# Transformer layer on one core: modulation columns summed over partitions by transposes and a VectorE reduction

## The chip, the cores and the metric

The kernel runs on one core of a Trainium2 chip. The metric is the time of one execution on the device in microseconds (us). Of the kernel before, three runs gave a median of 2660.23 us (2659.34 to 2661.08). The engines are called PE (TensorE, matmuls), PEld (its weight loads), DVE (VectorE), ACT (ScalarE), POOL (GpSimd) and SP (SyncE, which issues the DMAs here).

## The reference, cut to what matters

One layer works on 1024 latent tokens and 256 context tokens of width 1024: a half-step SwiGLU, two attentions side by side, a merge, another half-step SwiGLU. Every sub-layer is modulated by columns that come from two conditioning vectors, `c` for the latent tokens and `c_ctx` for the context tokens:

```python
m  = jnp.split((silu(c) @ w_ada + b_ada)[:, None, :], 9, axis=-1)   # w_ada: 1024 x 9216
mc = jnp.split(silu(c_ctx) @ w_ada + b_ada, 9, axis=-1)
...
x  = x + 0.5 * m[2] * rmsnorm(swiglu(rmsnorm(x) * (1 + m[1]) + m[0]))
```

Each `m[i]` is a vector-matrix product over 1024 rows of `w_ada`, 1024 outputs. `mc` is needed for i = 0 to 4 only, since the context tokens end in the attention. All of it is fp32.

## The kernel before, in words

Every large product of the kernel is done as three matmuls on a high and a low part of each fp32 operand (`mm3`), and the SwiGLU products are further cut into seven products of half size instead of eight (`Unit`, `Down7`). The program runs through a list of steps (`Plan`): `main` holds PE work, one step being for example 12 matmuls of 128x512, and `side` holds other work that is issued right behind a given main step. `plan.spread(steps, first, last)` lays a list of side steps evenly over the main steps `first` to `last`. The order so written is the order on every engine's queue; each engine takes its queue in order, and SP issues the loads and stores in the same order.

The modulation columns m = 0 and 1 are made at the start by PE (`Ada`). The others, m = 2 to 8, are made by DVE beside the large products (`AdaSum`). For one m, the weight rows are loaded in 16 pieces of 128x512 (k = 0 to 7, half h = 0 or 1). For each piece DVE multiplies by the conditioning value of the partition and adds to an accumulator `acc[v][h]` (v = 0 latent, v = 1 context, which only m < 5 has). After eight k an accumulator holds, for 512 outputs, 128 partial sums, one in each partition, and these must be added over the partitions and laid out as a column, output on the partition. That last step is `AdaSum.end`: in the kernel before it is one product per 128 outputs, with 128x128 of the accumulator as the weights and the column `ones` (part of the tile `strip`) as the moving operand; the result is one column of a PSUM bank `bv`. So m = 2, 3, 4 take 16 products each and m = 5 to 8 take 8 each, 80 in all. DVE then adds the bias `bada` and writes `mod[m]`.

`ada_steps` writes the side steps of some m: 18 steps with loads and accumulations, two empty ones, and `end`. m = 2 lies beside the first SwiGLU's up-products, m = 4 and 3 beside its down-products, m = 5, 6, 7 beside the projections that `lat_tile` makes, m = 8 beside the second SwiGLU's down-products.

PSUM has eight banks, in three tags: `bs` and `bm` with three buffers, `bv` with two. `bv` serves the fifth and third products of a `Unit` (`p5`, `p3`), two of eight tiles of `Down`, and `AdaSum.end`. `turn_` is a transpose on PE: `ident` is the identity, `x` the 128x128 block.

Of the kernel before, what the change touches and what calls it, by code (L numbers as in the profile page):

```python
# [12 lines left out]
ALU = mybir.AluOpType  # L13
AX = mybir.AxisListType

P = 128
# [5 lines left out]
KD = D // P  # L22
# [21 lines left out]
def hybrid_block(ctx: ExitStack, tc: tile.TileContext, a: dict, out: bass.AP):  # L44
# [11 lines left out]
    def nm(s):  # L56
        count[0] += 1
        return f"{s}_{count[0]}"
# [8 lines left out]
    def U(dt=F32, key="u"):  # L67
        return pools[key].tile([P, 1024], dt, tag="u", name=nm("x" + key))
# [7 lines left out]
    def T2(dt=F32, n=512):  # L76
        return pools["t"].tile([P, n], dt, tag="t", name=nm("t"))

    def ST(n=1):
        return sp.tile([P, n], F32, tag=f"st{n}", name=nm("st"))  # L80
# [7 lines left out]
    def PB(tag):  # L88
        return ps.tile([P, 512], F32, tag=tag, name=nm("b" + tag), bufs=PBUFS[tag])
# [8 lines left out]
    def const(name, shape, src=None, dt=F32):  # L98
        t = cp.tile(shape, dt, tag=name, name=name)
        if src is not None:  # L100
            ld(t, src)
        return t
# [4 lines left out]
    def pin(i):  # L107
        if pinned[0]:
            tc.keep_in_program_order(i)
        return i  # L110
# [39 lines left out]
    vec, act, pool = Engine(nc.vector), Engine(nc.scalar), Engine(nc.gpsimd)  # L150

    def mmul(o, s, m, start, stop):
        return pin(nc.tensor.matmul(o, s, m, start=start, stop=stop, skip_group_check=open_group[0]))  # L153

    def turn_(o, x, i):
        return pin(nc.tensor.transpose(o, x, i))  # L156
# [64 lines left out]
    ident = const("ident", [P, P])  # L221
    bada = const("bada", [P, 9, KD])
# [14 lines left out]
    ones = strip[:, 1:2]  # L237
# [7 lines left out]
    mod = [const(f"mod{m}", [P, 2, KD]) for m in range(9)]  # L245

    class Ada:
# [16 lines left out]
        def end(self):  # L264
            self.rows = T2()
            vec.tensor_copy(self.rows[:, :256], self.bank[:, :256])
            self.turn()
# [11 lines left out]
    class AdaSum(Ada):  # L279
# [16 lines left out]
                else:  # L296
                    vec.scalar_tensor_tensor(t[h], r, sc[:, k, v:v + 1], t[h], op0=ALU.mult, op1=ALU.add)

        def end(self):

            pb = PB("v")
            n = len(self.acc)
            for v, t in enumerate(self.acc):
                for k in range(KD):
                    mmul(pb[:, v * KD + k:v * KD + k + 1], t[k // 4][:, (k % 4) * P:(k % 4 + 1) * P], ones, True, True)
            for v in range(n):
                vec.tensor_tensor(mod[self.m][:, v, :], pb[:, v * KD:(v + 1) * KD], bada[:, self.m, :], op=ALU.add)

    cols = {}

    def ada_steps(ms):

        s = []
        cur = {}

        def step(m, k, h):
            if m not in cur:
                cur[m] = AdaSum(m)
            if k:
                cur[m].step(k - 1, h)  # L320
            if k < KD:
                cur[m].load(k, h)

        def end(m):
            cur[m].end()
            if m == 4:
                cols["a1"] = scale_col("a1", 4, 2, 2)
            if m == 7:
                cols["a2"] = scale_col("a2", 7, 4, 1)

        for m in ms:
            s += [lambda m=m, k=k, h=h: step(m, k, h) for k in range(KD + 1) for h in range(2)]
            s += [lambda: None] * 2 + [lambda m=m: end(m)]
        return s

    def scale_col(name, m, g, nv):
        t = const(name, [P, 2, KD])
        for v in range(nv):
            vec.scalar_tensor_tensor(t[:, v, :], mod[m][:, v, :], 1.0, ng[:, g, :], op0=ALU.add, op1=ALU.mult)
        return t  # L340
# [734 lines left out]
    e = len(plan.main)  # L1075
# [7 lines left out]
    rest1 = len(plan.main)  # L1083
    plan_rest(plan, units1)
    plan.spread(ada_steps((2,)), rest1 + 10, len(plan.main) - 10)


# [45 lines left out]
    for i, d in enumerate(downs):  # L1133
        last = i == len(downs) - 1
# [15 lines left out]
        e = len(plan.main)  # L1150
# [3 lines left out]
        if i < len(downs) - 2:  # L1154
            n = downs[i + 1]
            plan.spread([lambda n=n: n.loads(n.fs[0])], o, o + 1)
            plan.spread(n.steps(), o + 3, e)
        elif not last:
            n = downs[i + 1]
# [3 lines left out]
    for x, (p, f, w) in enumerate(ctx_at):  # L1163
# [3 lines left out]
        plan.spread([lambda f=f, w=w, e=e: ctx_split(f, w, e) for e in range(2)], q, max(q + 1, q1))  # L1167
    dstart = ctx_at[0][0] - 5
    plan.spread(ada_steps((4, 3)), dstart + 14, ctx_at[-4][0] - 6)

    gcol = {}
# [98 lines left out]
    e = len(plan.main)  # L1270
# [127 lines left out]
    for x, (c, s, ts) in enumerate(sets):  # L1398
# [5 lines left out]
        if x + 1 < len(sets):  # L1404
            plan.spread(sets[x + 1][1].loads(), o, o + 1)
            plan.spread(sets[x + 1][1].steps(), o + 1, len(plan.main))
    va_at = o
    plan.spread(ada_steps((5, 6, 7)), lat_at + 1, va_at - 2)

    def rotate(x, cc, ss, nh):  # L1410
# [470 lines left out]
    for e in range(2):  # L1881
        e = U(F32R)
# [204 lines left out]
    e = len(plan.main)  # L2087
# [118 lines left out]
```

## Time and profile before

| | |
|---|---|
| median of the runs shown | 2660.23 us |
| time of the profiled execution | 2662.05 us |
| its span in the profile | 2660.0 us |
| PE busy | 2609.1 us, 98% |
| PEld busy (beside PE) | 2234.1 us, 84% |
| DVE busy | 1847.5 us, 69% |
| ACT busy | 1171.9 us, 44% |
| mean granted PE clock | 0.994 |

The span is what the profile shows of the execution, 2.05 us less than the time of that execution. A row of the timeline gives the start, the length, the engine, the line, the operation and its tiles, how many instructions were merged into it, and in brackets the idle time ahead of it with what ended it. Buffer numbers are left out of the tile names. Matmuls overlap, so the time that a group of them takes on PE is read from its start to the start of the next group, not from its length. In rows of windows the number behind the engines' busy times is the granted PE clock, 1.00 being full speed. An fp32 matmul of `ones` appears as two passes (two weight loads and two matmuls), a transpose as one.

### The profile page before, as it was taken

What the parts mean: (1) busy time and instruction counts of PE and PEld (TensorE: products, weight loads), DVE (VectorE), ACT (ScalarE), POOL (GpSimd) and SP (SyncE); (2) the same over time, 40 slices, a digit from 0 to 9 for tenths busy, and PEclk for the clock granted to TensorE, in tenths of its full rate; (3) what the DMA queues carried; (4) which work ended last, traced back from release to release, by engine and by line L of the source; (5) the groups of instructions that cost most, each with busy time, mean ns of one, the idle gap of its engine ahead of it and who ended that gap; (6) DMA issues with size and microseconds to landing.
All of it is one profiled execution on the core that took longest, in us unless ns stands there. A gap on an engine that the chain in (4) does not pass through costs nothing.

```text
span 2660.0 us, 38323 instructions
## 1 busy us (share of the span) xinstructions
PE 2609.1 (98%) x13690; PEld 2234.1 (84%) x13690; DVE 1847.5 (69%) x3495; ACT 1171.9 (44%) x2248; POOL 227.9 (9%) x380
## 2 busy tenths in 40 slices
PE   7999999999999999999999999999999999999998
PEld 5888888888888788789888999998788888888887
DVE  4777875586866676675366998886625788778557
ACT  4532223531323663331355988875246422234533
POOL 0000000000000400000101432221011000000001
PEclk9999999999999999999999999999999999999999
DMA  7454433453433564477879953214224566546755
GB/s 287 154 165 147 140 123 106 141 171 113 160 111 119 185 217 168 159 246 227 234 269 271 258 142 74 74 30 171 99 92 167 185 238 229 186 167 246 276 184 196
DMA packets 220430, 460.58 MB, mean 173 GB/s; under 512 B 25488, under 2 KB 64592, under 8 KB 220240
## 3 DMA queue, kind: packets, MB, share of 16 engines
q1 hardware_dynamic: 220240, 458.14, 52.2%
q8 instruction: 108, 1.77, 0.3%
q14 instruction: 82, 0.67, 0.1%
HBM read 338.71 MB, written 119.34 MB: 172 GB/s over the span
## 4 chain that ended last, share of the span: by engine, by line
PE 53%; issue 33%; DVE 6%; ACT 5%; DMA 2%; POOL 1%; SPq 0%; DVEq 0%; POOLq 0%; ACTq 0%
PE bs L153 24%; PE bm L153 15%; PE bv L153 11%; PE bm L156 2%; ACT xu L1833 1%; DVE t L120 1%; DVE xu L1700 1%; DVE xv L120 1%; ACT t L120 1%; DVE xu L120 1%; POOL st L120 1%; ACT t L1859 1%; ACT xu L120 1%; DVE t L1860 1%; PE bs L156 1%
## 5 line engine op out<-in xcount | busy, mean ns | idle before, releaser
L153 PE MATMUL bm<-xu,xu 128*128 128x512 f32 (+1 forms) x2271 | 553.1, 388 | 1.4 <-DVE xu L120 1.1
L153 PEld LDWEIGHTS bm<-xu,xu 128*128 128x128 f32 x2271 | 419.8, 189 | 83.9 <-DVE xu L120 1.9
L153 PE MATMUL bs<-xu,xu 128*128 128x512 f32 (+1 forms) x1875 | 461.4, 386 | 0.5 <-DVE xu L120 0.4
L120 ACT CAST xu<-t 128x512 fp32r<-128x512 f32 x402 | 238.5, 617 | 388.9 <-DVE t L120 333.4
L153 PEld LDWEIGHTS bs<-xu,xu 128*128 128x128 f32 x1875 | 348.1, 189 | 68.2 <-DVE xu L120 0.8
L120 DVE TENSOR_TENSOR xu<-t,xu 128x512 fp32r<-128x512 f32 x402 | 265.7, 686 | 142.4 <-ACT xu L120 142.4
L153 PE MATMUL bs<-xv,xu 128*128 128x512 f32 (+1 forms) x1488 | 356.0, 389 | 5.1 <-DVE t L120 5.0
L153 PEld LDWEIGHTS bs<-xv,xu 128*128 128x128 f32 x1488 | 279.5, 189 | 63.0 <-issue 7.1
L153 PE MATMUL bv<-xv,xu 128*128 128x512 f32 x1276 | 318.5, 389 | 0.0
L153 PEld LDWEIGHTS bv<-xv,xu 128*128 128x128 f32 x1276 | 239.6, 188 | 49.8
L120 POOL TENSOR_SCALAR st<-st 128x1 f32<-128x1 f32 x72 | 37.8, 525 | 2077.6 <-ACT t L120 2017.9
L153 PE MATMUL bs<-w,w 96*128 96x512 f32 (+3 forms) x832 | 206.1, 366 | 7.7 <-DVE st L1725 7.1
L120 DVE TENSOR_TENSOR xu<-xu,xu 128x512 fp32r<-128x512 f32 (+2 forms) x219 | 149.3, 687 | 76.4 <-ACT xu L120 74.3
L153 PE MATMUL bm<-t,xu 128*128 128x256 f32 (+1 forms) x1272 | 167.4, 289 | 0.6 <-ACT t L120 0.4
L153 PEld LDWEIGHTS bm<-t,xu 128*128 128x128 f32 x1272 | 162.3, 193 | 5.7 <-ACT t L120 0.8
L120 DVE TENSOR_TENSOR xu<-xv,xu 128x512 fp32r<-128x512 f32 (+2 forms) x184 | 131.3, 738 | 48.1 <-ACT xu L120 45.0
L120 DVE TENSOR_TENSOR t<-t,t 128x512 f32<-128x512 f32 (+2 forms) x222 | 142.3, 642 | 25.8 <-ACT t L120 23.0
L153 PE MATMUL bv<-t,w 128*128 128x256 f32 x896 | 151.1, 288 | 5.0 <-ACT t L1859 1.7
L153 PEld LDWEIGHTS bv<-t,w 128*128 128x128 f32 x896 | 132.6, 189 | 20.6 <-DVE t L1860 4.9
L153 PE MATMUL bv<-xu,xu 128*128 128x512 f32 x530 | 143.4, 391 | 0.0
L120 ACT CAST xu<-xu 128x512 fp32r<-128x512 f32 (+2 forms) x211 | 127.9, 617 | 28.8 <-DMA xu<-in_wc 15.0
L153 PEld LDWEIGHTS bs<-w,w 96*128 96x128 f32 (+1 forms) x832 | 123.2, 190 | 17.1 <-DVE st L1725 10.1
(192 smaller groups left out, 3583.2 us busy)
## 6 DMA issues: line engine op xcount, KB each, us to landing
d<-t SPq DMA_DIRECT2D x321, 256.0 KB, 2.5
t<-d SPq DMA_DIRECT2D x204, 256.0 KB, 5.1
xu<-in_f1w SPq DMA_DIRECT2D x64, 512.0 KB, 4.1
xv<-in_f1w SPq DMA_DIRECT2D x64, 512.0 KB, 3.6
xu<-in_f2w SPq DMA_DIRECT2D x58, 512.0 KB, 4.6
t<-in_wada SPq DMA_DIRECT2D x112, 256.0 KB, 3.9
w<-d SPq DMA_DIRECT2D x112, 256.0 KB, 6.3
xv<-d SPq DMA_DIRECT2D x42, 512.0 KB, 5.4
```

The source lines that it names most:

```text
L120: return lambda *x, **y: pin(f(*x, **y))
L153: return pin(nc.tensor.matmul(o, s, m, start=start, stop=stop, skip_group_check=open_group[0]))
L156: return pin(nc.tensor.transpose(o, x, i))
L1700: nc.vector.tensor_scalar(dst, src, 1.0, FMIN, op0=ALU.mult, op1=ALU.max, accum_out=m)
L1833: nc.scalar.activation(x, x, AF.Exp, bias=n_[:, s:s + 1], accum_out=l[:, i:i + 1])
L1859: nc.scalar.copy(t[0], pb)
L1860: nc.vector.tensor_tensor(t[1], pb, f32(t[0]), op=ALU.subtract)
```

## The change

`AdaSum.end` takes one accumulator half at a time. Four transposes write the four 128x128 blocks of `acc[v][h]` into a `bv` bank, DVE sums each block along the free axis (`tensor_reduce`, 128x512 to 128x4) into a small tile `st`, and adds the bias into four columns of `mod[m]`. `ada_steps` makes a side step of each half: four for m = 2, 3, 4 and two for m = 5 to 8, where there was one. The lists of side steps grow from 21 to 24 (m = 2), 42 to 48 (m = 4, 3), 63 to 66 (m = 5, 6, 7) and 21 to 22 (m = 8), and each is still laid over the same main steps.

```diff
-        def end(self):
-            pb = PB("v")
-            n = len(self.acc)
-            for v, t in enumerate(self.acc):
-                for k in range(KD):
-                    mmul(pb[:, v * KD + k:v * KD + k + 1], t[k // 4][:, (k % 4) * P:(k % 4 + 1) * P], ones, True, True)
-            for v in range(n):
-                vec.tensor_tensor(mod[self.m][:, v, :], pb[:, v * KD:(v + 1) * KD], bada[:, self.m, :], op=ALU.add)
+        def end(self, v, h):
+            pb, s = PB("v"), ST(4)
+            for k in range(4):
+                turn_(pb[:, k * P:(k + 1) * P], self.acc[v][h][:, k * P:(k + 1) * P], ident)
+            vec.tensor_reduce(s, pb.rearrange("p (k c) -> p k c", k=4), axis=AX.X, op=ALU.add)
+            vec.tensor_tensor(mod[self.m][:, v, 4 * h:4 * h + 4], s, bada[:, self.m, 4 * h:4 * h + 4], op=ALU.add)
...
         for m in ms:
             s += [lambda m=m, k=k, h=h: step(m, k, h) for k in range(KD + 1) for h in range(2)]
-            s += [lambda: None] * 2 + [lambda m=m: end(m)]
+            ends = [(v, h) for v in range(2 if m < 5 else 1) for h in range(2)]
+            s += [lambda: None] * 2 + [lambda m=m, e=e: end(m, *e, e == ends[-1]) for e in ends]
```

On PE, at the end of m = 8 in the second SwiGLU's down-products (`bs` and `bm` with `xu` are those products, three to a row; the numbers only name tiles), the order before is:

```order
L153 MATMUL bs_23911<-xu_24325,xu_24322 128x512 x3
L153 MATMUL bm_23912<-xu_24325,xu_24322 128x512 x3
L153 MATMUL bv_24399<-strip,t_23960 128x1 x4
L153 MATMUL bv_24399<-strip,t_23961 128x1 x4
L153 MATMUL bs_23909<-xu_24348,xu_24345 128x512 x3
L153 MATMUL bm_23910<-xu_24348,xu_24345 128x512 x3
```

and now:

```order
L153 MATMUL bm_23969<-xu_24359,xu_24356 128x512 x3
L156 MATMUL bv_24434<-ident,t_24017 128x128 x4
L153 MATMUL bs_23966<-xu_24383,xu_24380 128x512 x3
L153 MATMUL bm_23967<-xu_24383,xu_24380 128x512 x3
L153 MATMUL bs_23968<-xu_24383,xu_24380 128x512 x3
L153 MATMUL bm_23969<-xu_24383,xu_24380 128x512 x3
L156 MATMUL bv_24464<-ident,t_24018 128x128 x4
```

The eight products with `strip` in one place have become two groups of four transposes, with a main step of twelve matmuls between them. For m = 2, 3 and 4 the sixteen products become four such groups, one to four main steps apart.

On DVE, at the end of m = 2 in the first SwiGLU's up-products, the order before is:

```order
L120 TENSOR_TENSOR xu_3499<-t_3481,xu_3499 128x512
L120 TENSOR_TENSOR xu_3502<-xu_3349,xu_3502 128x512
L120 TENSOR_TENSOR mod_102<-bv_3507,bada 128x8 x2
L120 TENSOR_TENSOR t_3556<-bs_3543,t_3540 128x512
L120 TENSOR_TENSOR t_3558<-xu_3349,t_3455 128x512
```

and at the first of the four new ends:

```order
L120 TENSOR_TENSOR t_3266<-bs_3253,t_3250 128x512
L120 TENSOR_TENSOR t_3268<-xu_3110,t_3185 128x512
L120 TENSOR_TENSOR xu_3270<-xu_3129,xu_3270 128x512
L120 TENSOR_REDUCE st_3274<-bv_3273 128x4
L120 TENSOR_TENSOR mod_102<-st_3274,bada 128x4
L120 TENSOR_TENSOR t_3309<-bv_3296,t_3250 128x512
```

The reduction of 512 elements per partition stands on DVE's queue four times where two additions of 8 elements stood once; the first row of the last piece already reads the PE step (`bs_3253`) behind which the transposes are placed.

More of the change, by code (lines that the diff above doesn't have):

```diff
@@ L322, in step, with end @@
                 cur[m].load(k, h)
-        def end(m):
-            cur[m].end()
-            if m == 4:
+        def end(m, v, h, last):
+            cur[m].end(v, h)
+            if last and m == 4:
                 cols["a1"] = scale_col("a1", 4, 2, 2)
-            if m == 7:
+            if last and m == 7:
                 cols["a2"] = scale_col("a2", 7, 4, 1)
```

## The prediction

> **What bounds the kernel now.** I read the page first: the busy times, the slices and the chain.
>
> ```profile
> PE 2609.1 (98%) x13690; PEld 2234.1 (84%) x13690; DVE 1847.5 (69%) x3495; ACT 1171.9 (44%) x2248; POOL 227.9 (9%) x380
> PE   7999999999999999999999999999999999999998
> PE 53%; issue 33%; DVE 6%; ACT 5%; DMA 2%; POOL 1%; SPq 0%; DVEq 0%; POOLq 0%; ACTq 0%
> ```
>
> PE is full in every slice but the first and last, and the chain runs over PE's own queue. So time taken off PE comes off the span, wherever it lies, unless PE then waits for what it did not wait for; time added to the others costs nothing as long as PE still finds its inputs. Second view: the products with the column of ones, by their tile.
>
> ```profile
> L153 PE MATMUL bv<-strip,t x176: 164/250/353, 86.0 to 2492.6; 128*128 128x1 f32 x176
>   DVE mod L120: 12.9, 7
> ```
>
> 176 passes are 88 fp32 products: 80 in the seven ends that change, 8 in `shift_cols`, which stays. The last row says who waited for them: DVE, 12.9 us in 7 waits; PE had no idle time ahead of them. Third view: PE's timeline around the ends.
>
> ```profile
> 419.22 2.88 PE L153 MATMUL bs<-xu,xu 128*128 128x512 f32 x12
> 421.94 4.21 PE L153 MATMUL bv<-strip,t 128*128 128x1 f32 x32
> 426.01 5.47 PE L153 MATMUL bm<-xu,xu 128*128 128x512 f32 x12
> 431.28 3.10 PE L153 MATMUL bs<-xv,xu 128*128 128x512 f32 x12
> 434.22 2.88 PE L153 MATMUL bm<-xu,xu 128*128 128x512 f32 x12
> ...
> 642.42 3.63 PE L153 MATMUL bv<-strip,t 128*128 128x1 f32 x32
> 645.91 2.29 PE L153 MATMUL bv<-xu,xu 128*128 128x512 f32 x6
> 648.00 2.51 PE L153 MATMUL bs<-xu,xu 128*128 128x512 f32 x6
> 650.35 1.53 PE L153 MATMUL bm<-xu,xu 128*128 128x512 f32 x6
> ...
> 786.46 3.63 PE L153 MATMUL bv<-strip,t 128*128 128x1 f32 x32
> 789.95 4.62 PE L153 MATMUL bm<-t,xu 128*128 128x256 f32 x24
> 797.15 3.04 PE L153 MATMUL bm<-t,xu 128*128 128x256 f32 x24
> ...
> 1194.53 3.33 PE L153 MATMUL bs<-xu,t 128*128 128x288 f32 x24
> 1197.70 1.84 PE L153 MATMUL bv<-strip,t 128*128 128x1 f32 x16
> 1199.40 3.41 PE L153 MATMUL bm<-xu,t 128*128 128x288 f32 x24
> 1202.64 4.00 PE L153 MATMUL bs<-xv,xu 128*128 128x352 f32 x24
> ...
> 2491.03 1.84 PE L153 MATMUL bv<-strip,t 128*128 128x1 f32 x16
> 2492.73 0.96 PE L153 MATMUL bs<-xu,xu 128*128 128x512 f32 x3
> 2493.52 0.85 PE L153 MATMUL bm<-xu,xu 128*128 128x512 f32 x3
> ```
>
> Two things are to be seen. An end of 16 products holds PE for 4.07 us (421.94 to 426.01) or 3.49 us, and one of 8 for 1.70 us. And the large matmuls behind an end of 16 are slow: twelve that otherwise take 2.72 us (419.22 to 421.94) take 5.27. The fourth view, windows, says why:
>
> ```profile
> 421.90:426.00 4.10, 4.10 (x33) 4.06 (x33) 3.87 (x7) 1.14 (x2) 0.00 (x0) 0.85 0.31 115
> 426.00:431.30 5.30, 5.30 (x14) 4.14 (x15) 0.24 (x2) 0.00 (x0) 0.00 (x0) 0.50 0.03 10
> 789.90:794.40 4.50, 4.50 (x26) 4.50 (x26) 0.24 (x2) 0.00 (x0) 0.00 (x0) 0.62 0.27 100
> 1199.40:1202.60 3.20, 3.20 (x26) 3.20 (x26) 0.17 (x1) 0.00 (x0) 0.00 (x0) 1.00 0.87 248
> ```
>
> The granted clock falls behind the ends of 16 (0.50 over the 5.3 us behind m = 2, a mean of 0.62 behind m = 3; behind m = 4 the matmuls slow down alike), and stays at 1.00 behind the end of 8 at 1197.70. So the 16-product ends cost twice, by themselves and by the clock.
>
> The Trainium skill ("TensorE: Matmul & The Clock Gate", Part 1) has the array fall to half its clock after an idle window of about 3.4 us; the rows agree on the length, but not on the word idle, since PE was executing throughout (4.10 of 4.10 us): 3.5 us of one-column products count as idle.
>
> **What is removed, from PE.** End by end, start to start, less what the large matmuls in the same stretch take at full clock:
> - m = 2: 421.94 to 434.22 is 12.28, less 2 x 2.72: 6.84 us.
> - m = 4: 642.42 to 650.35 is 7.93, less 2.72: 5.21 us.
> - m = 3: 3.49 for the products, and 4.62 instead of 3.04 for the group behind: 5.07 us.
> - m = 5: 1197.70 to 1202.64 is 4.94, less 3.17 (1194.53 to 1197.70): 1.77 us.
> - m = 8: 2491.03 to 2493.52 is 2.49, less 0.68 for three matmuls (a quarter of 2.72): 1.81 us.
> - m = 6 and 7 have the same 16 passes as m = 5; I take 1.79 each.
>
> Sum 24.3 us, of which the products are about 17.9 and the clock about 6.
>
> **What is added, on PE.** 80 transposes in groups of four, of which the order puts two groups back to back only at m = 6 and m = 7. The trace has such groups, made for the planes, inside the stream of large matmuls:
>
> ```profile
> 76.41 0.60 PE L156 MATMUL bs<-ident,xv 128*128 128x128 f32 x4
> 76.77 3.02 PE L153 MATMUL bm<-xu,xu 128*128 128x512 f32 x12
> 79.62 0.60 PE L156 MATMUL bs<-ident,xv 128*128 128x128 f32 x4
> ...
> 1301.05 0.60 PE L156 MATMUL bs<-ident,t 128*128 128x128 f32 x4
> 1301.48 0.60 PE L156 MATMUL bm<-ident,t 128*128 128x128 f32 x4
> 1301.84 3.00 PE L153 MATMUL bs<-xv,xv 128*128 128x512 f32 x12
> ...
> 76.40:86.00 9.60, 9.60 (x49) 7.99 (x48) 5.56 (x9) 4.86 (x8) 0.00 (x0) 1.00 0.52 170
> ```
>
> Four transposes and twelve matmuls repeat after 3.21 us (76.41 to 79.62), so a group costs 3.21 - 2.72 = 0.49 us; two groups together take 0.79 us themselves (1301.05 to 1301.84). 20 groups are 9.8 us, about 9.6 with the two pairs. The clock over three such rounds is 1.00, so no drop follows.
>
> The Trainium skill (the same page, Part 4) puts a transpose at about 275 ns in a kernel. Priced so, 80 of them are an estimated 22 us and nearly all of the gain is gone; the trace shows lengths that fit (the 0.60 us of four overlapped ones) but starts 0.09 us apart, and it is the starts that PE pays.
>
> **What is added, on DVE.** 20 reductions of 128x512 from PSUM, and 20 additions of 4 elements for 10 of 8. No such reduction is in the trace. Nearest rows:
>
> ```profile
> L120 DVE TENSOR_TENSOR t<-t,bs 128x512 f32<-128x512 f32 x112 | 76.5, 683 | 33.4 <-PE bs L153 33.3
> L1732 DVE TENSOR_REDUCE st<-st 128x2 f32<-128x4 f32 x32 | 4.8, 149 | 0.4
> L120 DVE TENSOR_TENSOR mod<-bv,bada 128x8 f32<-128x8 f32 x14 | 1.9, 163 | 13.9 <-PE bv L153 12.9 <-PE bv L156 1.1
> ```
>
> A reduction reads as many elements as the first row, and its output is as small as the second's: between 0.15 and 0.68 us. I take 0.68, since the rows of this kernel go by what is read. That makes 20 x 0.68 + 10 x 0.16 = 15.2 us more for DVE, none of it on PE's path by my sum. The cover is that DVE waits for PE in these stretches (33.3 us over the 112 additions of the first row), and stood waiting for the ones products themselves (12.9 us above). Each reduction stands on the queue behind a DVE instruction that reads the PE step just ahead of the transposes, so it waits only some 0.4 us for them (at m = 8 DVE reads no product in between and waits longer, as it does before). Behind it are queued the halves of weights that PE needs one to several steps (2.72 us each) later; a delay of 0.4 + 0.68 + 0.16 = 1.2 us stays below that. If the cover were gone, it would be 15 us (a rival below).
>
> **What moves.** Loads and accumulations are spread among 24 side steps where 21 were (66 where 63 were, 22 where 21 were), so each comes sooner, by an eighth of the stretch at most; their number, and that of the 112 loads of `in_wada` on SP's queue, is the same. A load stays two side steps ahead of its use. The 20 banks of `bv`, where 7 were, take turns with the products' own; the nearest reuse is that of a `Down` tile's bank two tiles and a group of transposes later, 2 x 1.36 + 0.49 = 3.2 us after its end, and DVE's addition that frees it takes 0.68 us. I cost both at nothing; a wait of one DVE instruction at every group would be 20 x 0.68 = 14 us at most.
>
> **Sum.** 24.3 - 9.6 = 14.7 us off the span of 2660.0. The profiled execution took 2662.05 us, 1.8 above the median of the runs; from the median 2660.2 I get 2645.5 us.
>
> What shakes it: the clock drops elsewhere too, behind short waits.
>
> ```profile
> 924.95 5.73 PE L153 MATMUL bm<-xu,t 128*128 128x512 f32 x24 [1.50 <-ACT t L120]
> 1120.27 4.57 PE L153 MATMUL bs<-xv,xu 128*128 128x512 f32 x12 [1.88 <-DVE t L120]
> ```
>
> After a wait of 1.88 us twelve matmuls took 4.57 instead of 2.88 us; after 1.50 us 24 took the usual time. Whether such a wait tips the clock looks like a matter of where it falls, and everything behind 422 us will now fall elsewhere: some two drops of 1.7 us more or fewer, so 3.4 us either way. The likeliest case's own range is 2641 to 2650.
>
> **Rivals.**
> - Slower: the transposes take the clock down, as one-column products do. The Trainium skill (same page, Part 4) says that transposes do not count as PE activity as other matmuls do. A drop costs at least 1.58 us (behind m = 3); behind all 20 groups that is 32 us, giving 2677, and it decides from the tenth group on (14.7 / 1.58 = 9.3). Against it: the 1.00 over the rounds of transposes above, and that 8 one-column products in 1.70 us did not drop it, four times as long as a group. Chance 0.03.
> - No change: DVE's 15.2 us, or the waits for banks, lie on PE's path, 2660. For it: PE sits at 98%, so any late input shows. Against it: DVE's waits for PE. Chance 0.05; the page's 275 ns for a transpose would land here too (24.3 - 22, 2658), and is in this chance.
> - Half the gain: the large matmuls behind m = 2, 4 and 3 are slow for another reason than the products ahead of them, and only those go: 17.9 - 9.6 = 8.3, 2652; a gain partly eaten by later waits ends here too. Chance 0.12.
> - The forecast: 0.80.
>
> **Numbers.** About 0.2% (5.3 us) is what a measurement of this kernel can tell from no change. The forecast and the half gain are both faster: 0.92; same 0.05; slower 0.03. The range of 2640 to 2653 holds the forecast with its clock drops and most of the half gain.
>
> **What would show it.** Right: no `strip` products behind 100 us, PE granted 1.00 throughout 420 to 435 and 640 to 655 us, 20 groups of four `ident,t` transposes that start some 0.4 us ahead of the next matmul, TENSOR_REDUCE rows of about 0.68 us, PE without idle time at the groups. Wrong: a clock of 0.5 behind a group, a wait of PE for `mod` or `st`, or PE rows of `bv` that wait for DVE.

## The result, and the profile after

The median is 2649.3 us (2647.57 to 2653.39, 6 runs) against 2661.37 us (2659.34 to 2663.9, 6 runs) before: 12.1 us less, ratio 0.9956 (95% interval 0.9944 to 0.9969). The profiled execution took 2648.12 us, its span is 2646.3 us, 13.7 us below the span before. The forecast was 2645.5 us, the range 2640 to 2653.

The page after, busy times:

```profile
PE 2596.5 (98%) x13610; PEld 2222.1 (84%) x13610; DVE 1861.2 (70%) x3525; ACT 1173.0 (44%) x2248; POOL 229.1 (9%) x380
```

PE has 12.6 us less to do, DVE 13.7 us more, and PE is as full as before. The groups of the reductions and of the transposes after (instructions, then us busy, mean ns, then idle time ahead):

```profile
L120 DVE TENSOR_REDUCE st<-bv 128x4 f32<-128x512 f32 x20 | 13.7, 685 | 5.1 <-PE bv L156 5.1
L156 PE MATMUL bv<-ident,t 128*128 128x128 f32 x84 | 12.5, 273 | 1.1 <-DVE t L120 1.1
```

The reduction takes 0.685 us. The 1.1 us of idle time at the transposes are at the four of `Ada` at the start (before 45 us); the 80 new ones have none. The timeline of PE after, at the first end of m = 2, and the granted clock where it had dropped, behind m = 2 and m = 4:

```profile
390.07 0.60 PE L156 MATMUL bv<-ident,t 128*128 128x128 f32 x4
390.43 2.99 PE L153 MATMUL bm<-xu,xu 128*128 128x512 f32 x12
393.26 2.88 PE L153 MATMUL bv<-xv,xu 128*128 128x512 f32 x12
...
424.10:432.00 7.90, 7.90 (x38) 6.59 (x37) 6.33 (x12) 2.25 (x4) 0.00 (x0) 1.00 0.18 66
640.00:648.00 8.00, 8.00 (x38) 6.62 (x37) 6.06 (x12) 0.00 (x0) 0.00 (x0) 1.00 0.27 100
```

A group costs 3.19 - 2.72 = 0.47 us, and the clock behind the ends is 1.00 (behind those of m = 3 too, 774 to 790 us). To see where the time went, both timelines are cut at rows that they share (the first and the last row of each list lie ahead of and behind all ends). Before:

```profile
86.02 1.84 PE L153 MATMUL bv<-strip,t 128*128 128x1 f32 x16
485.04 1.88 PE L153 MATMUL bm<-t,xu 128*128 128x256 f32 x6 [0.41 <-ACT t L120]
904.70 0.77 PE L156 MATMUL bs<-ident,xv 128*128 128x128 f32 x5 [3.44 <-ACT xv L120]
1137.61 4.58 PE L153 MATMUL bs<-xv,xu 128*128 128x512 f32 x12 [1.85 <-DVE t L120]
1361.76 1.64 PE L153 MATMUL bs<-xu,xu 128*128 128x512 f32 x6 [0.36 <-DVE xu L120]
2278.55 3.00 PE L153 MATMUL bs<-xv,xu 128*128 128x512 f32 x12 [0.38 <-DVE t L120]
2498.31 1.03 PE L156 MATMUL bv<-ident,st 128*128 128x128 f32 x8
```

After:

```profile
86.78 1.84 PE L153 MATMUL bv<-strip,t 128*128 128x1 f32 x16
480.88 1.88 PE L153 MATMUL bm<-t,xu 128*128 128x256 f32 x6 [0.43 <-ACT t L120]
894.07 1.33 PE L156 MATMUL bs<-ident,xv 128*128 128x128 f32 x5 [3.56 <-ACT xv L120]
1109.71 3.00 PE L153 MATMUL bs<-xv,xu 128*128 128x512 f32 x12 [1.89 <-DVE t L120]
1125.47 4.58 PE L153 MATMUL bs<-xv,xu 128*128 128x512 f32 x12 [1.88 <-DVE t L120]
1347.01 1.63 PE L153 MATMUL bs<-xu,xu 128*128 128x512 f32 x6 [0.36 <-DVE xu L120]
2265.80 2.97 PE L153 MATMUL bs<-xv,xu 128*128 128x512 f32 x12 [0.38 <-DVE t L120]
2484.65 1.03 PE L156 MATMUL bv<-ident,st 128*128 128x128 f32 x8
```

| stretch, what ends in it | before | after | change | forecast |
|---|---|---|---|---|
| shift_cols to 485 / 481: m = 2 | 399.02 | 394.10 | -4.92 | 6.84 - 4 x 0.49 = 4.88 |
| to 905 / 894: m = 4, 3 | 419.66 | 413.19 | -6.47 | 10.28 - 8 x 0.49 = 6.36 |
| to 1138 / 1125: none | 232.91 | 231.40 | -1.51 | 0 |
| to 1362 / 1347: m = 5, 6, 7 | 224.15 | 221.54 | -2.61 | 5.35 - 2.8 = 2.6 |
| to 2279 / 2266: none | 916.79 | 918.79 | +2.00 | 0 |
| to 2498 / 2485: m = 8 | 219.76 | 218.85 | -0.91 | 1.81 - 0.98 = 0.83 |

The four stretches with ends give 14.9 us where 14.7 were forecast. The rest is the ground between. Ahead of 86 us it is +0.8: there the clock is at 0.50 from 23.69 to 30.52 us, and before it was so for 3.41 us only. It is -1.5 where the clock used to drop behind a wait of 1.88 us at 1120 and now, behind the same wait at 1109.71, does not (3.00 instead of 4.57 us for twelve matmuls). And it is +2.0 between 1362 and 2279, where nothing was changed: the trace after has two clock drops there, at 1416.33 and 1805.45 us, and the trace before has none. At the first of them a wait of PE for ACT shrinks from 1.37 us to under 0.1, which makes up for it; the second costs about 1.5 us. The stretch of that second drop after, and the same place before (instructions in brackets):

```profile
1805.45:1808.86 3.41, 3.41 (x19) 3.41 (x18) 2.47 (x5) 1.81 (x5) 0.95 (x2) 0.50 0.00 0
...
1819.90:1823.31 3.41, 3.41 (x32) 3.41 (x31) 3.35 (x7) 2.75 (x6) 0.97 (x3) 1.00 0.01 2
```

### The profile page after: what moved, and what is told of

The parts are those of the page before. It is cut to its first block, busy times and chain, and to the rows that moved or that the text cites. A ratio compares the mean times of both kernels' runs of the same rounds, so it can differ in the third digit from the quotient of the medians.

```text
span 2646.3 us, 38182 instructions
## 1 busy us (share of the span) xinstructions
PE 2596.5 (98%) x13610; PEld 2222.1 (84%) x13610; DVE 1861.2 (70%) x3525; ACT 1173.0 (44%) x2248; POOL 229.1 (9%) x380
## 4 chain that ended last, share of the span: by engine, by line
PE 68%; issue 18%; DVE 6%; ACT 5%; DMA 2%; POOL 1%; SPq 0%; DVEq 0%; POOLq 0%; ACTq 0%
PE bs L153 31%; PE bm L153 19%; PE bv L153 15%; PE bm L156 2%; ACT xu L1832 1%; DVE t L120 1%; DVE xv L120 1%; DVE xu L1699 1%; DVE xu L120 1%; DMA w<-d 1%; ACT t L1858 1%; DVE t L1859 1%; PE bs L156 1%; ACT t L120 1%; POOL st L120 1%
```

## The experiments

Each was timed in four to eleven runs, beside the kernel before on the same chip; differences in us are the ratio's distance from 1 times the median of before beside it (2664.2, 2662.0 or 2661.7). The ratios are not quite those of the medians: by the medians alone the changed kernel, timed again, is 12.1 us below before where its ratio gives 13.3, and the last kernel 21.8 where its ratio gives 23.4.

**Only the ends of 16, or only those of 8.** In the first kernel `end` by transposes is used where `m < 5`, in the second where `m >= 5`; elsewhere the products stay.

> Only m = 2, 3, 4 (ends of 16 products) are done by transposes; m = 5 to 8 keep the products with ones. Theory (an end costs PE its own time and, if of 16, a clock drop behind it; DVE's reductions are hidden): 17.1 us of ends go and 12 groups of 0.47 us come, so 11.5 us less than before. Rival (the slow matmuls behind the 16-product ends have another cause): only the products' 11.05 us go, so 5.4 us less.

> Only m = 5 to 8 (ends of 8 products) are done by transposes; m = 2, 3, 4 keep the products. Theory: 7.2 us of ends go, 8 groups (3.6 us) come: 3.5 us less than before, and the clock drops behind m = 2, 4, 3 stay. Rival (DVE's added reductions cost PE something where DMA is busiest): nothing, or slower.

Measured: 0.9957 (0.9945 to 0.9970), 11.5 us less, and 0.9988 (0.9980 to 0.9997), 3.2 us less. Both are the theory's numbers. The interval of the first excludes the rival's 5.4 us (8.0 at the least), that of the second excludes no change, narrowly (0.8 us at the least). In the traces the first kernel has no clock drop at m = 2, 4 and 3, and the second still has all three, of 3.41 us each.

**The products kept, but in blocks of 8.** One side step for each `v`, no transposes (against the changed kernel, condensed):

```diff
-            ends = [(v, h) for v in range(2 if m < 5 else 1) for h in range(2)]
+            ends = [(v,) for v in range(2 if m < 5 else 1)]     # 8 products with ones in each
```

> No transposes at all: the products with ones stay, but the 16 of m = 2, 3, 4 are issued as two blocks of 8 (one for each v) in two side steps. Theory (a block of 3.5 us of one-column products drops the clock, one of 1.7 us does not): the three drops go, 6.1 us, less some 0.3 us for three more breaks in the stream: 5.8 us less than before, clock 1.00 at those places. Rival (the drop has another cause, or 8 products are enough when another 8 follow): no change, and the clock drops still.

Measured: 0.9971 (0.9960 to 0.9982), 7.7 us less (4.8 to 10.7). PE's timeline of this kernel at the two blocks of m = 2, and the clock over them and behind them:

```profile
410.82 1.84 PE L153 MATMUL bv<-strip,t 128*128 128x1 f32 x16
412.52 3.03 PE L153 MATMUL bv<-xv,xu 128*128 128x512 f32 x12
...
423.55 1.84 PE L153 MATMUL bv<-strip,t 128*128 128x1 f32 x16
425.25 3.03 PE L153 MATMUL bm<-xu,xu 128*128 128x512 f32 x12
...
410.80:412.50 1.70, 1.70 (x17) 1.68 (x16) 0.69 (x1) 0.00 (x0) 0.00 (x0) 1.00 0.00 0
412.50:418.00 5.50, 5.50 (x26) 4.54 (x26) 2.06 (x4) 0.00 (x0) 0.00 (x0) 1.00 0.68 215
```

The same products in the same number, and the clock no longer drops, at m = 4 and 3 neither. So some six tenths of what the change brought (7.7 of 12.1 to 13.3 us, with the interval above) need no transposes: it is the length of a block of one-column products, 3.5 us against 1.7, that set the clock.

**All transposes of an m in one place.** The groups of an m are issued in one side step (against the changed kernel):

```diff
+            for v in range(2 if m < 5 else 1):
+                for h in range(2):
+                    cur[m].end(v, h)
...
+            s += [lambda: None] * 2 + [lambda m=m: end(m)]
```

> Transposes and reductions as in the changed kernel, but all groups of an m in one side step, so 16 transposes in a row for m = 2, 3, 4. Theory: no clock drop from transposes; PE waits for DVE to empty a bv bank ahead of the third and fourth group (about 0.5 us each, six times), and saves some 0.1 us at each of 13 breaks: 1 to 3 us slower than the changed kernel, so 10 to 13 us less than before. Rival (it was the spreading that took the clock drops away): drops behind three blocks, 1.6 to 2.6 us each, so 5 to 7 us less than before.

Measured: 0.9991 (0.9982 to 1.0000), 2.4 us less: neither number. PE waits at each of the three ends of 16 transposes, 6.2 us in all, and the clock drops behind the waits of m = 2 and m = 3, but not behind the shortest, that of m = 4. PE's timeline of this kernel at m = 2, 4 and 3, DVE's at m = 2, and the clock behind m = 2 and behind m = 4:

```profile
421.02 1.03 PE L156 MATMUL bv<-ident,t 128*128 128x128 f32 x8
425.54 1.70 PE L156 MATMUL bv<-ident,t 128*128 128x128 f32 x8 [3.49 <-DVE st L120]
426.89 4.45 PE L153 MATMUL bm<-xu,xu 128*128 128x512 f32 x12
...
644.29 1.46 PE L156 MATMUL bv<-ident,t 128*128 128x128 f32 x8 [1.11 <-DVE st L120]
...
787.49 1.83 PE L156 MATMUL bv<-ident,t 128*128 128x128 f32 x8 [1.58 <-DVE st L120]
...
421.07 0.68 DVE L120 TENSOR_TENSOR xu<-t,xu 128x512 fp32r<-128x512 f32 x1
...
424.20 0.69 DVE L120 TENSOR_TENSOR xu<-xu,xu 128x512 fp32r<-128x512 f32 x1
424.80 0.68 DVE L120 TENSOR_REDUCE st<-bv 128x4 f32<-128x512 f32 x1
...
426.90:431.20 4.30, 4.30 (x15) 3.42 (x14) 1.20 (x4) 0.00 (x0) 0.00 (x0) 0.64 0.00 0
645.90:650.20 4.30, 4.30 (x19) 3.53 (x20) 2.47 (x7) 0.00 (x0) 0.00 (x0) 1.00 0.30 114
```

The third group needs the bank of the first, and the first reduction stands behind six other instructions on DVE (421.07 to 424.80). I had taken DVE to be one instruction behind; here its reduction starts 3.78 us after the first transpose (421.02 to 424.80). The next experiment takes that wait away and leaves the transposes in one place.

**The same with other banks.** `PB("v")` becomes `PB("vmsv"[2 * v + h])`.

> All groups of an m in one side step as in the version with the ends in one place, but the groups take banks of the tags bv, bm, bs, bv in turn instead of bv alone. Theory (what made that version slow was PE waiting for DVE, several instructions behind, to empty a bv bank, 3.49, 1.11 and 1.58 us, and the clock drops after these waits): most of the wait goes for groups two and three and shrinks for the fourth; 4 to 10 us less than before rather than 2.4. Rival (16 transposes in a row drop the clock by themselves): waits gone but clock 0.5 behind the three blocks, and no more than 5 us less than before.

Measured: 0.9949 (0.9935 to 0.9962), 13.6 us less: as good as the changed kernel, better than I expected. The waits at the ends are gone but for one of 0.24 us, and 16 transposes in a row are followed by matmuls at full clock, at all three places. The timeline of PE at m = 2:

```profile
422.89 0.60 PE L156 MATMUL bv<-ident,t 128*128 128x128 f32 x4
...
424.20 0.60 PE L156 MATMUL bv<-ident,t 128*128 128x128 f32 x4
424.55 2.99 PE L153 MATMUL bm<-xu,xu 128*128 128x512 f32 x12
427.38 2.88 PE L153 MATMUL bs<-xv,xu 128*128 128x512 f32 x12
```

So spreading the transposes is not what gains; where they share two banks it is what keeps PE from waiting for DVE.

**40 transposes in a row.** The last group of each m is issued ten times over (`list(range(4)) * 10`), 252 transposes more.

> The changed kernel with the last group of each m issued ten times over, 40 transposes in a row, 252 more in all. Theory (transposes stream 128 columns and keep the clock): 252 x 0.09 = 22.7 us slower than the changed kernel, clock 1.00 behind the blocks. Rival (transposes do not count as activity, as the Trainium skill's page TensorE: Matmul & The Clock Gate, Part 4, has it): blocks of 3.6 us drop the clock like the 16 products did, 1.6 to 2.6 us at each of seven places, so 34 to 41 us slower.

Measured: 1.0045 (1.0032 to 1.0057), 12.0 us more than before and 25.3 us more than the changed kernel timed beside it. PE's timeline of this kernel at m = 2, and the clock in the block and behind it:

```profile
423.50 4.53 PE L156 MATMUL bv<-ident,t 128*128 128x128 f32 x40
427.79 2.99 PE L153 MATMUL bm<-xu,xu 128*128 128x512 f32 x12
...
423.50:427.80 4.30, 4.30 (x42) 4.30 (x40) 3.83 (x7) 1.14 (x2) 0.00 (x0) 1.00 0.33 122
427.80:433.40 5.60, 5.60 (x28) 4.64 (x26) 0.85 (x2) 1.10 (x2) 0.00 (x0) 1.00 0.02 3
```

4.3 us of nothing but transposes leave the clock at 1.00, and so at the other six rows of 40; 3.5 us of one-column products took it to 0.50. In a long row a transpose takes 4.29 / 40 = 0.107 us, not 0.09, and 252 x 0.107 is 27 us. The Trainium skill ("TensorE: Matmul & The Clock Gate", Part 4) says that the full clock does not engage for transposes, since they do not count as PE activity in the same way. That is not what this trace shows: the transposes kept a clock that was full when they began. Whether they would raise it from 0.50, no run here shows. The figure of about 275 ns that the Trainium skill gives there fits the length of one transpose (273 ns in the row of the 84), but not what each costs where they follow each other.

**Three reductions for one.** Each `tensor_reduce` is issued three times.

> The changed kernel with every reduction on DVE issued three times, 40 more of about 0.68 us, 27 us of DVE time. Theory (DVE's part is hidden, what is short of the forecast is the clock elsewhere): within 1.5 us of the changed kernel. Rival (the missing 2.6 us are DVE's reductions on PE's path): 5 us slower than the changed kernel or more.

Measured: 0.9953 (0.9939 to 0.9967), 12.5 us less than before, where the changed kernel timed beside it has 13.3 less. DVE is busy 25.7 us more than in the changed kernel's profile (1886.9 against 1861.2 us), and the time grows by 0.8 us, inside what can be told from nothing. PE still has no wait at a group. DVE's part of the change is hidden.

**The changed kernel again.**

> The changed kernel once more, on the same chip as the three above. Theory: 12 to 14 us less than before, runs spread by some 5 us, and among its runs a longer span goes with a lower mean clock; if 14.7 us of PE work went, the rest must be found in the clock. Rival (a wait eats 2 to 3 us at the groups): its profile shows PE idle at the groups.

(The three named there are the versions with 40 transposes, with three reductions and with the sums off PE, which comes next.) Measured: 0.9950 (0.9938 to 0.9963), 13.3 us less (9.8 to 16.5). PE has no wait at the groups, so the rival is out. The part on the clock came out only in part. In the first set of the changed kernel's runs the longest span goes with the lowest mean clock (2651.6 us at 0.993) and the shortest with the highest (2645.7 at 0.996); in this set the shortest (2646.0 us) has 0.995, and the highest, 0.996, belongs to 2647.3 us. The profile of this set has the two drops between 1362 and 2279 us too (at 1415.20 and 1804.32).

**The sums off PE.** Since DVE's work is hidden and PE's is not, the next step is to take the transposes off PE as well. DVE transposes the accumulator in 32x32 blocks and sums each block, which leaves for each output four partial sums, one in each quarter of the partitions; one small matmul per m with a matrix of stacked identities adds them.

```diff
+            vec.transpose(x, self.acc[v][h])
+            vec.tensor_reduce(self.sums[:, o:o + 16], x.rearrange("p (j i) -> p j i", i=32), axis=AX.X, op=ALU.add)
...
+            mmul(pb[:, 0:n], self.fold, self.sums[:, 0:n], True, True)      # n = 64 or 32, once for each m
```

> The partition sums leave PE almost wholly: DVE transposes the accumulator in 32x32 blocks and sums each block, which leaves four partial sums per output, one in each quarter of the partitions; one small matmul per m (128x64 or 128x32, with a fold matrix that POOL makes) adds the four, and DVE adds the bias. Theory (PE's queue is what counts): 9.4 us of transposes go, seven ends of about 0.3 us come, 7 us faster than the changed kernel, though DVE gets some 16 us more. Rival (DVE has no room for more): no faster.

Measured: 0.9959 (0.9946 to 0.9972), 10.9 us less than before, no faster than the changed kernel (13.3 less beside it). The rival was right for one stage: at m = 5, 6 and 7, whose side steps are densest, PE stood in front of the small matmul until DVE had made the sums. PE's timeline of this kernel, and the clock behind the second of them:

```profile
1183.89 0.38 PE L153 MATMUL bv<-t 128*128 128x32 f32 x2 [1.63 <-DVE t L120]
1215.92 0.61 PE L153 MATMUL bv<-t 128*128 128x32 f32 x2 [3.82 <-DVE t L120]
1252.87 0.45 PE L153 MATMUL bv<-t 128*128 128x32 f32 x2 [2.65 <-DVE t L120]
...
1216.30:1220.00 3.70, 3.70 (x14) 3.70 (x14) 0.65 (x4) 0.00 (x0) 0.00 (x0) 0.50 0.92 272
```

8.1 us of waits, and a clock drop behind each of the three. Two ways out: keep transposes there, or issue the small matmul later.

> Block sums on DVE with one small matmul for m = 2, 3, 4, transposes as in the changed kernel for m = 5 to 8. Theory: 12 groups of 0.47 us go from PE and three matmuls of 0.3 us come, 4.7 us faster than the changed kernel, so 17 to 18 us less than before, and no wait of PE at an end. Rival (DVE has no room): as fast as the changed kernel or slower.

> The version with 32x32 block sums on DVE and one small matmul per m, but the matmuls of m = 5 and 6 are issued six side steps into the next m, and that of m = 7 six empty steps later, so that PE no longer stands in front of a matmul whose sums DVE has not made. Theory (there PE waited 8.1 us in the three ends and lost some 5 us of clock behind them): 7 us faster than the changed kernel, so some 20 us less than before. Rival (DVE falls behind anyway where it has projections to copy out): waits of PE stay, no faster than the changed kernel.

```diff
+            if held is not None:
+                new.insert(6, lambda m=held: end(m))       # the matmul of m = 5, 6 among the steps of the next m
...
+        s += [lambda: None] * (6 if m == 7 else 2) + [lambda m=held: end(m)]
```

The code of the late version moves more than that: the matmul of m = 4 too goes six steps into m = 3, and those of m = 2, 3 and 8 come two empty steps later than in the version before it.

Measured: 0.9925 (0.9912 to 0.9937), 20.0 us less, with transposes kept for m = 5 to 8; and 0.9912 (0.9898 to 0.9925), 23.4 us less than before (median 2639.89 us, 4 runs), with the late matmuls. Both are more than the theory's 17 to 18 and 20 us, which their intervals still hold (16.8 to 23.4, and 20.0 to 27.2). The second beats both kernels: its interval lies below both that were measured for the changed kernel, though that one was not timed beside it. PE's timeline of it at m = 2 and m = 6:

```profile
425.23 0.33 PE L153 MATMUL bv<-t 128*128 128x64 f32 x2
425.37 3.02 PE L153 MATMUL bs<-xv,xu 128*128 128x512 f32 x12
428.22 2.88 PE L153 MATMUL bm<-xu,xu 128*128 128x512 f32 x12
...
1210.78 0.30 PE L153 MATMUL bv<-t 128*128 128x32 f32 x2
```

At m = 2 an end now costs PE 2.99 - 2.72 = 0.27 us, and PE has no wait at any of the seven.

## Why the prediction was right, point by point

- **PE bounds, and what leaves its queue leaves the span.** Right: the ends' stretches shrank by 14.9 us in the profiles, 14.7 forecast, and PE waits at none of the 20 groups. Taking the transposes off PE as well brought some 10 us more by the same rule, where 7 were expected.
- **The ends of 16 cost the clock too.** Right, and the term that mattered: the three ends of 16 gave 11.5 us alone, of which the clock is about 6, and splitting their products in blocks of 8 gave 7.7 us (4.8 to 10.7) without a transpose.
- **A group of transposes at 0.49 us.** 0.47 measured. That they keep the clock was argued from rounds of four; the row of 40 shows it.
- **The reduction at 0.68 us, hidden.** 0.685 us, and hidden even three times over. DVE is busy 13.7 us more, 15.2 were forecast.
- **Banks and waits at nothing.** Right for the changed kernel, but for a weaker reason than I gave. The reading that a reduction waits only some 0.4 us for its transposes, with a delay of 1.2 us in all, was wrong: in the changed kernel itself the second group of m = 2 ends at 402.02 us and its reduction starts at 405.24, 3.22 us later. The bound, one DVE instruction of 0.68 us at each group, was too small as well: with the groups in one place the waits were 3.49, 1.11 and 1.58 us. The changed kernel is spared since its groups are one to four main steps apart, or, at m = 6 and 7, only two in a row, one for each bank.
- **The sum.** 14.7 us forecast, 12.1 measured by the medians (8.3 to 14.9 by the interval), 13.7 between the two profiled spans. The step that was mis-sized is the clock's drops elsewhere, which the sum had at zero and the range at 3.4 us either way: in the two profiled executions one drop fewer behind the waits near 1115 us, two more between 1362 and 2279 and a longer one at the start came to 1.2 us against the change. The range allowed for them; that they nearly cancelled in these two profiles is luck. Between the medians I have no account by stretches, and the mean clocks of the runs, which follow the spans in one set and not in the other, do not give one. A small slip besides: by its own rows a pair of groups costs 0.79 + 0.13 = 0.92 us, which makes 9.7 us for all, not 9.6.

## What to carry to other kernels

Where one engine's queue is full, price a step by the start of the next instruction on that queue and look at the granted clock for some microseconds behind it: here about 6 of the 17.1 us that the ends of 16 products cost lay in the large matmuls that followed. Keep matmuls with one column in short blocks between large ones (1.70 us was short enough here; nothing between that and 3.5 was tried), and move small reductions to an engine that has room, even if it needs more time for them there. Then place the instruction of the full engine that takes the result far enough behind: the sums on DVE were no faster than the transposes with the small matmul right behind them, and some 10 us faster with it a few steps later.

## What the runs showed of the hardware that was not expected

- One-column fp32 products are poor activity for the clock: 3.5 us of them took the granted clock to 0.50 with PE executing throughout, 1.7 us did not, and 4.3 us of transposes did not.
- A wait of PE of the same length may or may not be followed by a clock drop. The waits at the same two places of the program lasted 1.88 and 1.85 us before (to 1120 and 1138 us), and both were followed by one; after, they lasted 1.89 and 1.88 us (to 1110 and 1125 us), and only the second was. The traces hint at what decides. Every drop ahead of the kernel's end lasts 3.41 or 6.83 us, and before, from 400 us on, they start whole multiples of 3.413 us apart (424.81, 646.67, 790.03, 906.09, 1121.13 and 1138.19 us: 65, 42, 34, 63 and 5 of them), as if the clock were set anew at the end of each such stretch. The first wait lay in one stretch before (first row) and was cut by the end of one after (the other two; 1126.20 us, where the next drop starts, is five stretches later than 1109.13):

```profile
1117.72:1121.13 3.41, 1.53 (x7) 0.96 (x7) 2.90 (x5) 1.32 (x3) 0.00 (x0) 1.00 0.43 159
...
1105.72:1109.13 3.41, 2.10 (x10) 1.40 (x8) 1.54 (x4) 2.29 (x4) 0.00 (x0) 1.00 0.41 154
1109.13:1112.54 3.41, 2.83 (x12) 2.36 (x13) 3.41 (x6) 0.62 (x1) 0.00 (x0) 1.00 0.78 233
```

PE was busy 1.53 us of the one stretch, and 2.10 and 2.83 us of the two. The ends of 16 fit the same reading: their products take 2.9, 2.7 and 3.3 us of the stretch ahead of their drop, and a block of 8 cannot take more than 1.70. It is not the whole account, since in the last kernel PE is busy 1.57 us of the stretch from 1118.29 to 1121.71 and no drop follows; no run was made to test it.
